# Chunk inverses on diagonal blocks of 64, one piece of expert weights split ahead, last residual by an accumulating DMA

## The chip, the core and the metric

The kernel runs on one core of a Trainium2 chip. The metric is the device time of one execution in microseconds. Before the change it is 3314.12 us, the median of 3 runs (3313.49 to 3316.09). The core has TensorE (PE; its weight loads are listed apart as PEld), VectorE (DVE), ScalarE (ACT), GpSimd (POOL) and SyncE (SP, which issues most transfers).

## The reference, cut to what matters

Two blocks run one after the other on 512 tokens of width 1024: the first has two layers (mixers, cross-attention, a gated feed-forward), the second a mixer and a layer of 32 experts. The change touches the RWKV mixer of the first block, and the start and the end of the expert layer.

```python
def rwkv7_chunked(r, log_w, k, v, a_vec, b_vec):
    ...
    A_ab = pair(a_dec, b_inv, strict)      # strictly lower triangle, inside one chunk
    A_ak = pair(a_dec, k_inv, strict)
    A_rb = pair(r_dec, b_inv, incl)
    A_rk = pair(r_dec, k_inv, incl)
    rhs = jnp.concatenate([a_dec, jnp.einsum('bhnls,bhnsv->bhnlv', A_ak, v)], axis=-1)
    sol = lax.linalg.triangular_solve(jnp.eye(L, dtype=F32) - A_ab, rhs, ...)
    ...
    def step(S, inp):                      # over the chunks, state S
        ...

def moe_ffn(h, w_router, b_router, w1, b1, w2, b2):
    logits = (xt @ w_router + b_router).astype(jnp.float32)
    top_v, top_i = lax.top_k(logits, TOP_K)
    gate = jax.nn.softmax(top_v, axis=-1)
    ...
    def expert_block(args):
        xb, e = args
        hid = xb @ w1[e] + b1[e]
        return swiglu_clamped(hid) @ w2[e] + b2[e]
    ...
# in second_block
        x = x + gate2 * moe_ffn(h2, w_router[l], b_router[l], w1[l], b1[l], w2[l], b2[l])
    return rms_norm_2(x, normf_w)
```

## The kernel before, in words

Everything is emitted by one program whose order on each engine is fixed when it is built: `merge` (L276) draws from generators in proportion to the weights that stand beside them, and the framework then places the instructions on the engines. On each engine they run in that order, and each waits for what it needs.

**The RWKV mixer.** Its 8 heads are handled in 4 pairs, p = 0 to 3. `rwkv_front(p)` makes the decayed operands `adec`, `binv`, `kinv`, `rdec` (128 partitions, 64 for each head of the pair, 512 tokens wide) from three dense products with streamed weights (`acc<-x,whi` and `acc<-x,wlo`). `rwkv_back(p)` (L773) turns them into the output. While the back of pair p runs, the front of pair p+1 is merged into it; the back of pair 3 is merged with the keys and values of the cross-attention (`mem_kv`; its products are `acc<-mp,...` and `pv<-...,mp`).

The kernel works on chunks of 64 tokens. A tile of 128 tokens holds two chunks, so a 128x128 matrix of products between the tokens of a tile has two wanted 64x64 blocks on its diagonal; the rest is removed by masks. The triangular solve is done by an inverse of (I - A) built up by doubling, for each of the two heads e of the pair apart:

- `pair` (L788): four products of 64 partitions, 128x128 each, give A (`Am`) and its transpose; both are copied by a mask into X and P, which start as identities.
- Five levels l: `prod` (L799) is four products of 128x128. Q = (Am P) masked on DVE (L846), P += X Q (L852), and, but for the last level, X += Q X (L854). So a level has two chains, one for each head, that run in turn on PE and DVE.
- `rest` (L825) is other work of the back that `next(rest, None)` hands out between the levels: `pA<-adec,kinv`, `pv`, `pA<-rdec,...`.
- Then pz = P R for each head (`pp<-R,XP`), ACT copies it out, and seven state steps (`pS`), `pw`, `py` and a norm follow.

**The expert layer.** Weights come as pieces of 128x2048 (1 MB). A piece is split into `whi` (a cast on ACT) and `wlo` (a subtraction on DVE), by `halves` (L2012); `prepare(n)` (L2024) splits until n pieces stand ready. `early` (L1938) calls `prepare(2)` after the routing and before the first tokens have been gathered and turned into `xh` and `xl`. PE multiplies a piece in 12 matmuls (`hid<-whi,xh`, `hid<-whi,xl`, `hid<-wlo,xh`, four of each kind; the down products `y` likewise). `run` (L2129) chains the instructions of PE, DVE and ACT in the order in which they are written.

**The end.** The results of experts 0 to 29 have been added to `zD` in DRAM by scatters on POOL; the results of 30 and 31 are spread to the tokens by selection matrices S. `residual` (L2214) loads the residual `xrD` and `zD` for four tiles of 128 tokens. `sums` (L2228) multiplies `zD` by the gate `g2B` on DVE. `begin` (L2274) starts a PSUM tile: residual times identity, output biases by the gates, expert 30. `gather_late` (L2290) adds expert 31 and then adds the PSUM tile to the multiplied `zD` on DVE (L2296). `norm` (L2325) squares, takes the root, scales and stores. `begin` runs for tiles 0 to 2 before the result of expert 31 is there, and for tile 3 after the first `gather_late`.

Of the kernel before, what the change touches and what calls it, by code (L numbers as in the profile page):

```python
# [182 lines left out]
def constants():  # L183
# [14 lines left out]
    for l in range(6):  # L198
# [3 lines left out]
        lev.append(off.astype(np.float32))  # L202
    A["cm"] = np.ascontiguousarray(np.concatenate(
        [ident, bones, bsw, m_incl, m_incl_sw, m_strict_sw, lev[0]] + [x.T for x in lev], axis=1))
    seg = np.ones((128, 512), np.float32)
    seg[:, ::64] = 0.0
    A["seg64"] = seg
# [74 lines left out]
class Net:  # L282
# [363 lines left out]
    def rwkv_lora(self):  # L646

        nc, A = self.nc, self.A
        self.vz = []
        for j in range(2):  # L650
            t = self.per.tile([128, 4, 192], F32, name=f"vz{j}")
            nc.gpsimd.memset(t[:, :, 64:128], 0.0)
            self.vz.append(t)
        self.wa2, self.wg2, self.lr, self.sgl = self.four("lora")
        self.yb = self.four("y")
        nc.sync.dma_start(self.wa2, A["rw_wa2"])
        nc.sync.dma_start(self.wg2, A["rw_g2"])
        lr = self.shift(self.dense(A["w_ab"], 8, 8, self.x), self.v("mu_lr1"), "lr", self.lr)
        nc.scalar.activation(lr[:64], lr[:64], AF.Tanh)
        yield 5  # L660
        sgl = self.shift(self.dense(A["w_ab"], 9, 8, self.x), self.v("mu_lr2"), "sgl", self.sgl)
        nc.scalar.activation(sgl, sgl, AF.Sigmoid)
        yield 5
# [109 lines left out]
    def rwkv_back(self, p, d, y):  # L773
# [9 lines left out]
        idb = b4(self.ident)  # L783
        rr = [slice(64 * e, 64 * e + 64) for e in range(2)]
        hc = [slice(64 - 64 * e, 128 - 64 * e) for e in range(2)]
        tiles = [slice(i * 128, i * 128 + 128) for i in range(4)]
# [9 lines left out]
            TT(t4(t), t4(ps), b4(self.c(mask)), op=OP.mult)  # L796
            return t

        def prod(x, z):  # L799
            ps = self.px("pp")  # L800
            for s in tiles:
                self.mm(ps[:, s], x[:, s], z[:, s])
            return ps


        Am, X, P = [], [], []
        inv = self.four("XP")
        pairs = self.four("Arb")
        for e in range(2):
            x, pt_ = inv[2 * e:2 * e + 2]  # L810
            nc.scalar.copy(t4(x), idb)
            nc.scalar.copy(t4(pt_), idb)
            ps = pair(e, adec, binv)
            am = self.f("Am")
            nc.scalar.copy(am, ps)
            nc.vector.copy_predicated(t4(x), b4(self.c("lev0").bitcast(I32)), t4(ps))
            ps = pair(e, binv, adec)
            nc.vector.copy_predicated(t4(pt_), b4(self.c("levt").bitcast(I32)), t4(ps))
            Am.append(am)
            X.append(x)  # L820
            P.append(pt_)
            yield 1.7
        Arb, Ark = [None, None], [None, None]

        def rest():  # L825
# [13 lines left out]

        rest = rest()  # L840
        for l in range(1, 6):
            Q = [None, None]
            for e in range(2):
                pq = prod(Am[e], P[e])
                Q[e] = self.f("Q")
                TT(t4(Q[e]), t4(pq), b4(self.c("levt", l)), op=OP.mult)  # L846
                yield 0.9
            for e in range(2):
                pp = prod(X[e], Q[e])
                if l < 5:  # L850
                    px = prod(Q[e], X[e])
                TT(P[e], pp, P[e], op=OP.add)  # L852
                if l < 5:
                    TT(X[e], px, X[e], op=OP.add)  # L854
                yield 1.7
                next(rest, None)
        for _ in rest:
            yield 0.9
        Z = []
        ZS = self.f("ZS")  # L860
        for e in range(2):
            pz = prod(P[e], R[e])
            z = self.f("Z")
            nc.scalar.copy(t4(ZS)[:, :, rr[e]], t4(pz)[:, :, rr[e]])
            nc.scalar.copy(z, pz)
            for c in range(2):
                nc.scalar.copy(ZV[rr[c], :, c, hc[e]], t4(pz)[rr[c], :, hc[e]])
            Z.append(z)
            yield 0.9
# [1049 lines left out]
class Moe:  # L1919
# [18 lines left out]
    def early(self):  # L1938

        self.wctx = ExitStack()  # L1940
        self.ctx.push(self.wctx)
        self.w = [self.wctx.enter_context(self.tc.tile_pool(name=f"mw{j}", bufs=1, side="right")) for j in range(2)]
        self.pieces = 0
        self.ready = []
        self.prepare(2)

    def open(self):
        nc, A = self.nc, self.A
# [196 lines left out]
    def experts(self):  # L2145
# [46 lines left out]
        acc, z = self.residual()  # L2192
        first = self.spread(ys[30][1], where[0])
        add = [[lambda i=i: self.sums(z[i])] for i in range(4)]
# [5 lines left out]
        p = [self.begin(i, acc[i], gT[0], first) for i in range(3)]  # L2200
        last = self.spread(self.scaled(31, sl[31], y)[1], where[1])
        norm = None
        for i in range(4):
            if i == 1:
                p.append(self.begin(3, acc[3], gT[0], first))
# [8 lines left out]
    def residual(self):  # L2214

        nc = self.nc
        t = [self.big("xr") for _ in range(5)]
        acc = [t[i // 2][:, i % 2 * 1024:i % 2 * 1024 + 1024] for i in range(4)]
        z = [t[3 + i // 2][:, i % 2 * 1024:i % 2 * 1024 + 1024] for i in range(4)]
        self.nf = t[2][:, :1024]  # L2220
        for i in range(4):
            nc.sync.dma_start(acc[i], self.n.xrD[i * 128:i * 128 + 128])
# [3 lines left out]
        return acc, z  # L2226

    def sums(self, z):  # L2228
        self.nc.vector.tensor_tensor(z, z, self.g2, op=OP.mult)

    def results(self, zD, i, big):
        z = [t for _ in range(2) for b in (big("z"),) for t in (b[:, :1024], b[:, 1024:])]
# [38 lines left out]
            self.split(hi[:, s], lo[:, s], ys[:, s])  # L2271
        return S, hi, lo

    def begin(self, i, xr, gT, late):  # L2274

        if i in (1, 2):
            pool, tag = ((self.py, "y"), (self.pt, "pt"))[i - 1]
            p = [pool.tile([128, 512], F32, tag=tag, name="pz") for _ in range(2)]
        else:
            p = self.ph.tile([128, 1024], F32, tag="hid", name="pz")  # L2280
            p = [p[:, :512], p[:, 512:]]
        S, hi, lo = late
        for o, s in zip(p, (slice(0, 512), slice(512, 1024))):
            self.mm(o, self.ident, xr[:, s], True, False)
            self.mm(o, gT[:96, i * 128:i * 128 + 128], self.b[1][:96, s], False, False)
            self.mm(o, S[:, i, :], hi[:, s], False, False)
            self.mm(o, S[:, i, :], lo[:, s], False, False)
        return p
# [51 lines left out]
def emit(ctx, tc, A, upto="all", dbg=None):  # L2340
# [26 lines left out]
    N.early()  # L2367
    N.clear(N.zD, N.big("zero"))
    for p in range(4):
        back = (N.rwkv_back(p, d[p], y), 45)  # L2370
        if p < 3:
            merge(back, (N.rwkv_front(p + 1, d[p + 1]), 27))
        else:
# [62 lines left out]
```

## Time and profile before

| | |
|---|---|
| median of 3 runs | 3314.12 us |
| the profiled execution: its own time | 3308.96 us |
| its span | 3307.1 us |
| PE busy | 3216.8 us (97%) |
| DVE busy | 2347.8 us (71%) |
| ACT busy | 1832.9 us (55%) |
| RWKV backs of the four pairs, from their first product to the end of the last inverse | about 160 to 460 us of the span |
| expert layer | about 2098 to 3274 us of the span |

The span is the time from the first to the last instruction; the 1.9 us beside it lie around it. Busy time of matmuls is modelled at their ends, so the distance between the starts of one block and the next is a better price than the length of a row. fp32 matmuls leave two records each: 160 products `pp<-Q,XP` of 128x128 stand as x320. Rows name tiles by their output and inputs and carry the line of the helper that recorded them (L348 is `mm` of the first block, L1981 that of the expert layer).

### The profile page before, as it was taken

Reading aid. Unit: us, or ns where it says so; the run is one execution under the profiler, and the core shown is the slowest. Engines: PE = TensorE matmul, PEld = TensorE weight load, DVE = VectorE, ACT = ScalarE, POOL = GpSimd, SP = SyncE. Lnnn points to the kernel's source line nnn. Section 1 sums busy time; section 2 is a strip of 40 time slices with the busy share of each in tenths; the row PEclk is TensorE's granted clock in tenths of the full one; section 3 lists DMA queues with packets and bytes.
Section 4 is the critical chain, followed back from the end, with each engine's and each line's share of the span. In section 5 each row is a group of like instructions: output and inputs, shape, how many; then the busy total and the mean of one; then the engine's idle time right before and its main releaser. Section 6 shows DMA issues by size and latency. Waiting matters only on the chain. (4 is left out here: it accounts for less than half of the span.)

```text
span 3307.1 us, 40569 instructions
## 1 busy us (share of the span) xinstructions
PE 3216.8 (97%) x15334; PEld 2564.3 (78%) x15335; DVE 2347.8 (71%) x3023; ACT 1832.9 (55%) x2356; POOL 205.4 (6%) x139
## 2 busy tenths in 40 slices
PE   8999999999999999999999998899999999999997
PEld 6688887777876787777877765688888888788885
DVE  5677765577634665577634354799999999999997
ACT  6643334443425864443434355577777777777774
POOL 1000001100000001100011000100110010111000
PEclk9999999999999999999999999899999999999999
DMA  5201123344333234345334312799999999999994
GB/s 167 79 20 29 43 89 121 122 168 169 90 125 111 75 118 126 126 147 184 90 110 135 128 50 105 275 355 360 366 366 366 353 358 367 359 358 357 369 358 161
DMA packets 152967, 649.61 MB, mean 196 GB/s; under 512 B 21335, under 2 KB 26543, under 8 KB 103228
## 3 DMA queue, kind: packets, MB, share of 16 engines
q1 hardware_dynamic: 143836, 630.86, 52.3%
q0 software_dynamic: 8928, 16.09, 1.9%
q8 instruction: 122, 2.00, 0.2%
q14 instruction: 81, 0.66, 0.1%
HBM read 626.55 MB, written 36.75 MB: 201 GB/s over the span
## 5 line engine op out<-in xcount | busy, mean ns | idle before, releaser
L1990 DVE TENSOR_TENSOR wlo<-w,whi 128x2048 fp32r<-128x2048 f32 x384 | 868.2, 2288 | 81.2 <-ACT whi L1989 76.5
L1989 ACT CAST whi<-w 128x2048 fp32r<-128x2048 f32 x384 | 729.7, 1908 | 295.9 <-PE hid L1981 178.5
L348 PE MATMUL acc<-x,whi 128*128 128x512 f32 (+1 forms) x2656 | 861.9, 404 | 7.2 <-ACT x L420 2.6
L383 ACT CAST whi<-raw 128x512 fp32r<-128x512 f32 (+1 forms) x578 | 352.8, 613 | 727.8 <-PE acc L348 600.6
L384 DVE TENSOR_TENSOR wlo<-raw,whi 128x512 fp32r<-128x512 f32 (+1 forms) x578 | 394.2, 685 | 389.8 <-ACT whi L383 373.5
L348 PEld LDWEIGHTS acc<-x,whi 128*128 128x128 f32 (+1 forms) x2656 | 496.1, 188 | 155.3 <-issue 25.4
L348 PE MATMUL acc<-x,wlo 128*128 128x512 f32 (+1 forms) x1328 | 534.0, 402 | 0.0
L1981 PE MATMUL hid<-whi,xh 128*128 128x512 f32 x1024 | 412.5, 403 | 4.5 <-DVE ln L2084 4.5
L1981 PE MATMUL hid<-whi,xl 128*128 128x512 f32 x1024 | 402.5, 393 | 2.6 <-DVE xl L1990 2.6
L348 PEld LDWEIGHTS acc<-x,wlo 128*128 128x128 f32 (+1 forms) x1328 | 250.0, 188 | 66.1 <-issue 6.3
L1981 PE MATMUL hid<-wlo,xh 128*128 128x512 f32 x1024 | 278.2, 393 | 0.0
L1981 PEld LDWEIGHTS hid<-whi,xh 128*128 128x128 f32 x1024 | 193.8, 189 | 46.2 <-issue 5.5
L1981 PEld LDWEIGHTS hid<-wlo,xh 128*128 128x128 f32 x1024 | 193.5, 189 | 42.7
L1981 PEld LDWEIGHTS hid<-whi,xl 128*128 128x128 f32 x1024 | 194.0, 189 | 41.7 <-DVE xl L1990 3.1
L1981 PE MATMUL y<-whi,ah 128*128 128x512 f32 x512 | 200.8, 392 | 0.7 <-ACT ah L1989 0.7
L1981 PE MATMUL y<-whi,al 128*128 128x512 f32 x512 | 200.3, 391 | 0.9 <-DVE al L1990 0.9
L348 PE MATMUL acc<-act,whi 128*128 128x512 f32 x512 | 162.6, 398 | 0.0
L1981 PE MATMUL y<-wlo,ah 128*128 128x512 f32 x512 | 158.8, 391 | 0.5 <-DVE wlo L1990 0.5
L455 POOL TENSOR_TENSOR sq<-sq,hs 128x512 f32<-128x512 f32 x42 | 56.2, 1339 | 1207.5 <-ACT hs L454 1207.1
L2121 POOL DMA_INDIRECT zD<-ys,sl x30 | 79.0, 2634 | 776.2 <-ACT sel L2043 466.5
L348 PEld LDWEIGHTS acc<-act,whi 128*128 128x128 f32 x512 | 95.2, 188 | 27.0 <-issue 5.1
L1981 PEld LDWEIGHTS y<-whi,ah 128*128 128x128 f32 x512 | 96.1, 188 | 22.6 <-ACT ah L1989 1.1
(651 smaller groups left out, 4653.7 us busy)
## 6 DMA issues: line engine op xcount, KB each, us to landing
w<-in_w_dram SPq DMA_DIRECT2D x384, 1024.0 KB, 8.2
raw<-in_w_up_dram SPq DMA_DIRECT2D x86, 512.0 KB, 3.5
wada<-in_w_ada_dram SPq DMA_DIRECT2D x96, 256.0 KB, 5.0
raw<-in_w_dn_dram SPq DMA_DIRECT2D x32, 512.0 KB, 3.6
h<-hD SPq DMA_DIRECT2D x48, 256.0 KB, 2.8
raw<-in_w_ab_dram SPq DMA_DIRECT2D x22, 512.0 KB, 3.6
hD<-hn SPq DMA_DIRECT2D x40, 256.0 KB, 2.0
raw<-in_w_k_dram SPq DMA_DIRECT2D x16, 512.0 KB, 3.5
```

The costliest lines, as they stand in the source:

```text
L348: self.nc.tensor.matmul(out, l, r, start=start, stop=stop)
L383: nc.scalar.copy(hi[:, :w], raw[:, c:c + w])
L384: nc.vector.tensor_tensor(lo[:, :w], raw[:, c:c + w], hi[:, :w].bitcast(F32), op=OP.subtract)
L455: nc.gpsimd.tensor_tensor(self.sq, self.sq, s, op=OP.add)
L1981: self.nc.tensor.matmul(out, l, r, start=start, stop=stop)
L1989: self.nc.scalar.copy(hi, src)
L1990: self.nc.vector.tensor_tensor(lo, src, hi.bitcast(F32), op=OP.subtract)
L2121: self.nc.gpsimd.indirect_dma_start(out=self.n.zD, out_offset=bass.IndirectOffsetOnAxis(ap=sl[:, 0:1], axis=0), in_=ys, in_offset=None, bo ...
```

## The change: what it does

Three edits.

1. The inverse keeps the 64x64 diagonal blocks alone, both heads side by side: one tile of 128 partitions (chunk c of a tile on partitions 64c to 64c+63) by 512 columns (8 blocks of 64: 4 tiles of head 0, 4 of head 1). A product is now 16 products of 64x64, whose operands and output lie on partitions 0 to 63 or 64 to 127 in turn; one chain takes the place of two. pz becomes 8 products of 64 partitions by 128 columns for each head. The masks come in a new small tile `cmc`, loaded in `rwkv_lora`. The weight of the back in the merge goes from 45 to 32.
2. `early` splits one piece of weights ahead in place of two.
3. The residual is no longer multiplied by the identity on PE; after `sums` has multiplied a tile, a DMA issued by POOL adds `xrD` to it.

```diff
+        t8 = lambda t: t.rearrange("p (i l) -> p i l", l=64)
+        cm = lambda j, n: self.cmc[:, 64 * j:64 * j + 64].unsqueeze(1).to_broadcast([128, n, 64])
+        cols = [slice(j * 64, j * 64 + 64) for j in range(8)]
+        half = [slice(256 * e, 256 * e + 256) for e in range(2)]
+        def pair_c(x, z):
+            ps = [self.px("pA") for _ in range(2)]
+            for i in range(4):
+                for c in range(2):
+                    t = slice(128 * i + 64 * c, 128 * i + 64 * c + 64)
+                    for e in range(2):
+                        self.mm(ps[e][rr[c], cols[i]], x[rr[e], t], z[rr[e], t])
+            return [t[:, :256] for t in ps]
-        def prod(x, z):
+        def prod_c(x, z):
             ps = self.px("pp")
-            for s in tiles:
-                self.mm(ps[:, s], x[:, s], z[:, s])
+            for s in cols:
+                for c in range(2):
+                    self.mm(ps[rr[c], s], x[rr[c], s], z[rr[c], s])
             return ps
...
         for l in range(1, 6):
-            Q = [None, None]
-            for e in range(2):
-                pq = prod(Am[e], P[e])
-                Q[e] = self.f("Q")
-                TT(t4(Q[e]), t4(pq), b4(self.c("levt", l)), op=OP.mult)
-                yield 0.9
-            for e in range(2):
-                pp = prod(X[e], Q[e])
-                if l < 5:
-                    px = prod(Q[e], X[e])
-                TT(P[e], pp, P[e], op=OP.add)
-                if l < 5:
-                    TT(X[e], px, X[e], op=OP.add)
-                yield 1.7
-                next(rest, None)
+            pq = prod_c(Am, P)
+            Q = self.f("Q")
+            TT(t8(Q), t8(pq), cm(2 + l, 8), op=OP.mult)
+            yield 0.9
+            next(rest, None)
+            pp = prod_c(X, Q)
+            if l < 5:
+                px = prod_c(Q, X)
+            TT(P, pp, P, op=OP.add)
+            if l < 5:
+                TT(X, px, X, op=OP.add)
+            yield 1.7
+            next(rest, None)
...
         for e in range(2):
-            pz = prod(P[e], R[e])
+            pz = self.px("pp")
+            for i, s in enumerate(tiles):
+                for c in range(2):
+                    self.mm(pz[rr[c], s], P[rr[c], cols[4 * e + i]], R[e][rr[c], s])
...
-        self.prepare(2)
+        self.prepare(1)
...
-    def sums(self, z):
+    def sums(self, z, i):
         self.nc.vector.tensor_tensor(z, z, self.g2, op=OP.mult)
+        self.nc.gpsimd.dma_start(out=z, in_=self.n.xrD[i * 128:i * 128 + 128], accum_op=OP.add)
...
-            self.mm(o, self.ident, xr[:, s], True, False)
-            self.mm(o, gT[:96, i * 128:i * 128 + 128], self.b[1][:96, s], False, False)
+            self.mm(o, gT[:96, i * 128:i * 128 + 128], self.b[1][:96, s], True, False)
...
-        back = (N.rwkv_back(p, d[p], y), 45)
+        back = (N.rwkv_back(p, d[p], y), 32)
```

How the order moves is shown at three places. In the order the sizes are those of the output, and xN counts instructions (an fp32 matmul is one here).

PE, second and third level of pair 0, before (`pp<-XP,Am` is Am P, `pp<-Q,XP` is X Q, `pp<-XP,Q` is Q X; `pn` is work of the front of pair 1, `pA` and `pv` are `rest`):

```order
L348 MATMUL pv<-vz_332,aak 128x128 x4
L348 MATMUL pp<-XP,Am 128x128 x8
L348 MATMUL pp<-Q,XP 128x128 x4
L348 MATMUL pp<-XP,Q 128x128 x4
L348 MATMUL pn<-k2s,cm 128x512
L348 MATMUL pA<-adec,kinv 128x128 x4
L348 MATMUL pp<-Q,XP 128x128 x4
L348 MATMUL pp<-XP,Q 128x128 x4
```

The same place now:

```order
L351 MATMUL pv<-vz_332,aak 128x128 x4
L351 MATMUL pp<-XP,Am 64x64 x16
L351 MATMUL pA<-adec,kinv 128x128 x4
L351 MATMUL pp<-Q,XP 64x64 x16
L351 MATMUL pp<-XP,Q 64x64 x16
L351 MATMUL pn<-k2s,cm 128x512
L351 MATMUL pv<-vz_332,aak 128x128 x4
L351 MATMUL pp<-XP,Am 64x64 x16
```

Where products of one head stood between Am P and X Q of the other, there is now a product of `rest`.

DVE at the start of the expert layer, before (`di` is the last result of the routing, `wlo` a piece of weights, `xl` the first tokens):

```order
L1888 CAST di<-ds 128x16
L1990 TENSOR_TENSOR wlo<-w,whi 128x2048 x2
L1964 MEMSET meps 128x1
L1990 TENSOR_TENSOR xl<-pt,xh 128x512 x2
L1990 TENSOR_TENSOR wlo<-w,whi 128x2048
L2303 TENSOR_REDUCE mxc<-cnt 1x1
```

The same place now:

```order
L1907 CAST di<-ds 128x16
L2009 TENSOR_TENSOR wlo<-w,whi 128x2048
L1983 MEMSET meps 128x1
L2320 TENSOR_REDUCE mxc<-cnt 1x1
L2009 TENSOR_TENSOR xl<-pt,xh 128x512 x2
L2009 TENSOR_TENSOR wlo<-w,whi 128x2048 x3
```

One piece has moved from ahead of the tokens to behind them, and a small reduction the other way.

PE at the end, one half of a `begin`, before:

```order
L1981 MATMUL pz<-xr,ident__78 128x512
L1981 MATMUL pz<-b_16468,gT 128x512
L1981 MATMUL pz<-yh,S 128x512
L1981 MATMUL pz<-yl,S 128x512
```

The same place now:

```order
L2000 MATMUL pz<-b_16866,gT 128x512
L2000 MATMUL pz<-yh,S 128x512
L2000 MATMUL pz<-yl,S 128x512
```

The identity is gone from all eight halves; the order of DVE there is the same as before.

## Rows read from the trace of the kernel before

**Rows 1.** The page, part 1: busy time of each engine.

```profile
PE 3216.8 (97%) x15334; PEld 2564.3 (78%) x15335; DVE 2347.8 (71%) x3023; ACT 1832.9 (55%) x2356; POOL 205.4 (6%) x139
```

**Rows 2.** By stretches: width, then busy us of each engine, clock, DMA.

```profile
160.00:465.00 305.00, 299.88 (x2193) 263.20 (x2192) 212.25 (x372) 114.38 (x207) 0.00 (x0) 1.00 0.13 40
2060.00:3240.00 1180.00, 1161.06 (x5356) 955.87 (x5355) 1080.40 (x853) 859.48 (x676) 120.26 (x66) 0.99 0.92 353
```

**Rows 3.** What PE waited for, 160 to 465 us: total, times, longest.

```profile
PE pp L348 <- DVE Q L846: 2.3, 1, 2.3
```

**Rows 4.** Groups on PE by shape, 160 to 465 us: busy us, mean ns.

```profile
L348 PE MATMUL pp<-Q,XP 128*128 128x128 f32 x320 | 44.8, 283 | 2.3 <-DVE Q L846 2.3
...
L348 PE MATMUL pp<-R,XP 128*128 128x128 f32 x64 | 8.3, 278 | 0.0
```

**Rows 5.** Timeline of PEld inside pair 0: start us, us, what.

```profile
186.89 1.87 PEld L348 LDWEIGHTS pp<-XP,Am 128*128 128x128 f32 x16
188.68 0.19 PEld L348 LDWEIGHTS acc<-x,wlo 128*128 128x128 f32 x1
```

**Rows 6.** Timeline of PEld at products of 64x64, three places, 88 to 229 us.

```profile
88.58 0.85 PEld L348 LDWEIGHTS pkv<-vt,ket 64*64 64x64 f32 x28 [0.37 <-ACT ket L557]
...
95.01 0.31 PEld L348 LDWEIGHTS po<-qd,S 64*64 64x64 f32 x8
...
228.10 1.06 PEld L348 LDWEIGHTS py<-reff,S 64*64 64x64 f32 x20
```

**Rows 7.** Instructions on the tile po: ns min/median/max.

```profile
L348 PEld LDWEIGHTS po<-qd,S x112: 129/133/135, 92.7 to 157.1; 64*64 64x64 f32 x112
```

**Rows 8.** Timeline of PEld at a change of shape, 173 to 175 us.

```profile
173.65 0.96 PEld L348 LDWEIGHTS pA<-adec,kinv 64*128 64x128 f32 x8
...
174.73 0.97 PEld L348 LDWEIGHTS pp<-Q,XP 128*128 128x128 f32 x8
```

**Rows 9.** Timeline from a product to the next level's, 177 to 179.5 us.

```profile
177.41 1.87 PEld L348 LDWEIGHTS pp<-XP,Am 128*128 128x128 f32 x16
...
178.61 0.69 DVE L846 TENSOR_TENSOR Q<-pp,cm 128x512 f32<-128x512 f32 x1 [1.09 <-PE pp L348]
```

**Rows 10.** Timeline at the start of the expert layer, 2096 to 2107.5 us.

```profile
2096.24 4.49 DVE L1990 TENSOR_TENSOR wlo<-w,whi 128x2048 fp32r<-128x2048 f32 x2
2097.36 1.32 ACT L1989 CAST xh<-pt 128x512 fp32r<-128x512 f32 x2 [4.81 <-PE pt L2007]
...
2101.39 0.80 PE L1981 MATMUL hid<-whi,xl 128*128 128x512 f32 x1 [2.59 <-DVE xl L1990]
...
2106.25 0.63 PE L1981 MATMUL hid<-whi,xh 128*128 128x512 f32 x1
...
2107.02 0.39 PE L1981 MATMUL hid<-whi,xh 128*128 128x512 f32 x1
```

**Rows 11.** Timeline of the end, 3272 to 3295 us.

```profile
3272.15 4.62 DVE L2229 TENSOR_TENSOR xr<-xr,g2B 128x1024 f32<-128x1024 f32 x4
...
3274.03 0.42 PEld L1981 LDWEIGHTS pz<-xr,ident__78 128*128 128x128 f32 x2
...
3274.69 0.19 PEld L1981 LDWEIGHTS pz<-b,gT 96*128 96x128 f32 x1 [0.24 <-issue]
...
3278.12 1.35 DVE L1990 TENSOR_TENSOR yl<-ys,yh 128x512 fp32r<-128x512 f32 x2
...
3283.39 0.19 PEld L1981 LDWEIGHTS pz<-yh,S 128*128 128x128 f32 x1
...
3284.27 0.69 DVE L2296 TENSOR_TENSOR xr<-xr,pz 128x512 f32<-128x512 f32 x1 [4.80 <-PE pz L1981]
...
3289.42 1.28 DVE L2296 TENSOR_TENSOR xr<-xr,pz 128x512 f32<-128x512 f32 x2 [2.89 <-PE pz L1981]
```

**Rows 12.** DMA issues: KB each, median us from issue to landing.

```profile
raw<-in_w_up_dram SPq DMA_DIRECT2D x86, 512.0 KB, 3.5
...
zD<-ys,sl POOLq DMA_INDIRECT x30, 12.2
```

More of the change, by code (lines that the diff above doesn't have):

```diff
@@ L204, in constants @@
         [ident, bones, bsw, m_incl, m_incl_sw, m_strict_sw, lev[0]] + [x.T for x in lev], axis=1))
+    A["cmc"] = np.ascontiguousarray(np.concatenate(
+        [np.concatenate([x[:64, :64], x[64:, 64:]]) for x in [ident, lev[0]] + [x.T for x in lev]], axis=1))
     seg = np.ones((128, 512), np.float32)
@@ L655, in rwkv_lora @@
         self.yb = self.four("y")
+        self.cmc = self.f("cmc")
+        nc.sync.dma_start(self.cmc, A["cmc"])
         nc.sync.dma_start(self.wa2, A["rw_wa2"])
@@ L797, in masked @@
             return t
-        def prod(x, z):
+        t8 = lambda t: t.rearrange("p (i l) -> p i l", l=64)
[11 more added lines that the diff above has]
+        def prod_c(x, z):
             ps = self.px("pp")
-            for s in tiles:
-                self.mm(ps[:, s], x[:, s], z[:, s])
+            for s in cols:
+                for c in range(2):
+                    self.mm(ps[rr[c], s], x[rr[c], s], z[rr[c], s])
             return ps
-        Am, X, P = [], [], []
         inv = self.four("XP")
+        X, P = inv[:2]
         pairs = self.four("Arb")
+        Am = self.f("Am")
+        for t in (X, P):
+            nc.scalar.copy(t8(t), cm(0, 8))
+        ps = pair_c(adec, binv)
         for e in range(2):
[L810 to L821, printed above, removed]
-            yield 1.7
+            nc.scalar.copy(Am[:, half[e]], ps[e])
+            nc.vector.copy_predicated(t8(X[:, half[e]]), cm(1, 4).bitcast(I32), t8(ps[e]))
+        yield 1.7
+        ps = pair_c(binv, adec)
+        for e in range(2):
+            nc.vector.copy_predicated(t8(P[:, half[e]]), cm(2, 4).bitcast(I32), t8(ps[e]))
+        yield 1.7
         Arb, Ark = [None, None], [None, None]
@@ L841, in rwkv_back @@
         for l in range(1, 6):
-            Q = [None, None]
-            for e in range(2):
-                pq = prod(Am[e], P[e])
-                Q[e] = self.f("Q")
-                TT(t4(Q[e]), t4(pq), b4(self.c("levt", l)), op=OP.mult)
-                yield 0.9
-            for e in range(2):
-                pp = prod(X[e], Q[e])
-                if l < 5:
-                    px = prod(Q[e], X[e])
-                TT(P[e], pp, P[e], op=OP.add)
-                if l < 5:
-                    TT(X[e], px, X[e], op=OP.add)
-                yield 1.7
-                next(rest, None)
+            pq = prod_c(Am, P)
[9 more added lines that the diff above has]
+                TT(X, px, X, op=OP.add)
+            yield 1.7
+            next(rest, None)
         for _ in rest:
@@ L2191, in experts @@
             self.fetch()
-        acc, z = self.residual()
+        z = self.residual()
         first = self.spread(ys[30][1], where[0])
-        add = [[lambda i=i: self.sums(z[i])] for i in range(4)]
+        add = [[lambda i=i: self.sums(z[i], i)] for i in range(4)]
         y = self.ph.tile([128, 1024], F32, tag="hid", name="y31")
@@ L2199, in experts @@
         self.nc.scalar.activation(t, self.g2[:, 1023:], AF.Sqrt, scale=0.0, bias=self.eps)
-        p = [self.begin(i, acc[i], gT[0], first) for i in range(3)]
+        p = [self.begin(i, gT[0], first) for i in range(3)]
         last = self.spread(self.scaled(31, sl[31], y)[1], where[1])
@@ L2204, in experts @@
             if i == 1:
-                p.append(self.begin(3, acc[3], gT[0], first))
+                p.append(self.begin(3, gT[0], first))
             self.gather_late(z[i], p[i], i, last)
@@ L2216, in residual @@
         nc = self.nc
-        t = [self.big("xr") for _ in range(5)]
-        acc = [t[i // 2][:, i % 2 * 1024:i % 2 * 1024 + 1024] for i in range(4)]
-        z = [t[3 + i // 2][:, i % 2 * 1024:i % 2 * 1024 + 1024] for i in range(4)]
+        t = [self.big("z") for _ in range(3)]
+        z = [t[i // 2][:, i % 2 * 1024:i % 2 * 1024 + 1024] for i in range(4)]
         self.nf = t[2][:, :1024]
-        for i in range(4):
-            nc.sync.dma_start(acc[i], self.n.xrD[i * 128:i * 128 + 128])
         nc.sync.dma_start(self.nf, self.A["normf"].to_broadcast([128, 1024]))
@@ L2225, in residual @@
             nc.sync.dma_start(z[i], self.n.zD[i * 128:i * 128 + 128])
-        return acc, z
-    def sums(self, z):
+        return z
+    def sums(self, z, i):
         self.nc.vector.tensor_tensor(z, z, self.g2, op=OP.mult)
+        self.nc.gpsimd.dma_start(out=z, in_=self.n.xrD[i * 128:i * 128 + 128], accum_op=OP.add)
     def results(self, zD, i, big):
@@ L2272, in spread, with begin @@
         return S, hi, lo
-    def begin(self, i, xr, gT, late):
+    def begin(self, i, gT, late):
         if i in (1, 2):
```

1 line of the change is left out of this document (removed).

## The prediction

> **What bounds the kernel now.** I read the page's busy times first: PE 97%, DVE 71%, ACT 55% [rows 1]. The average could hide stages with another limit, so the two stretches that hold the three edits come next, by windows [rows 2]. In the RWKV backs (160 to 465 us) PE is busy 299.88 of 305.00 us at clock 1.00, DVE 212. In the expert layer (2060 to 3240 us) PE is busy 1161 of 1180 us, with the DMA share at 0.92. So what comes off PE's list comes off the end, unless PE then waits. In the backs the waits of PE name one long one on the inverse, 2.3 us for a Q, once [rows 3]: two heads in turn keep it fed. Last I read the timeline of weight loads (PEld), since the distance from one block's start to the next prices a product, and the two places of edits 2 and 3.
>
> **Edit 1, what goes.** The groups by shape give each product as two records: `pp<-Q,XP` x320, pz x64 [rows 4]. By the code a pair has 112 matmuls of 128x128 in the levels (24 in four levels, 16 in the fifth), 8 for pz and 16 for A and its transpose: 136, in four pairs 544, or 1088 records. Sixteen records of Am P start at 186.89, the next block at 188.68 [rows 5]: 0.112 us each. 1088 x 0.112 = 122 us off PE.
>
> **Edit 1, what comes.** 16 matmuls of 64x64x64 for each of 14 products, and 32 for A and its transpose: 256 a pair, 1024 in all, 2048 records. pz is 64 matmuls of 64 rows by 128 columns, 128 records. A record has half the columns of the old one and there are twice as many, so this pays only if records on different parts of the array overlap. The trace has three blocks of 64x64 to price that [rows 6], the last record of each taken as 0.133 us long [rows 7]:
> - `po`, one row half and both column halves, 64 columns: (0.31 - 0.133)/7 = 25 ns a record.
> - `pkv`, all four quarters: (0.85 - 0.133)/27 = 27 ns.
> - `py`, one quarter only: (1.06 - 0.133)/19 = 49 ns.
>
> The new products alternate between two quarters, as `po` does, though on two row halves. I take 25 ns: 2048 x 25 = 51.2 us. pz, with twice the columns, at 53 ns: 6.8 us. The upper end is `py`, 49 ns.
>
> What only this change adds is PE changing between full-size and 64-row work. At such a change 8 records take 1.08 us from start to start (173.65 to 174.73 [rows 8]) where 8 x 0.112 = 0.89 is due, so 0.19 us. Along the order I count 81 changes before and 160 now: 79 x 0.19 = 15 us. Bounds: 0 (the 0.19 may be the pipeline's own) to twice that.
>
> Waits: one chain now has no other head to fill the time from Am P to X Q. From its issue end DVE still needs about 1.05 us: Am P's block of 16 records is replaced at 177.41 + 1.79, its Q of 0.69 us starts at 178.61 and, for one head, waits 1.09 us on PE [rows 9]; so the last record's drain, 0.69 of DVE and two handovers stand between the products. The new order puts `pA<-adec,kinv`, `pv` or a dense product of the front between them, most of them about 0.9 us or more, so I charge only the levels where the filler is short: 4.5 us in all. The bounds are 0 and 26 us (20 levels, each 1.05 for Q and 0.25 for P, nothing covering).
>
> DVE gets lighter: per pair 28 tensor operations of 0.69 us become 14, so it bounds nothing. ACT loses half its identity copies. The weight 32 for 45 only sets which front instructions stand between levels; it is in the counted order. The new 256 KB load of `cmc` stands on SP's queue among the first loads of weights, where SP waits for free buffers; a 512 KB load lands in 3.5 us [rows 12], so it costs 0, at most 1 us.
>
> Sum: -122 + 51.2 + 6.8 + 15 + 4.5 = **-44 us** (own bounds -56, with half the changes' price and no waits, to -33).
>
> The Trainium skill, "TensorEngine Tiling (Array Packing)", section "Restrictions and Gotchas", speaks against this: row tiles that run at one time may not share a PSUM bank. `prod_c` writes both partition halves from both row halves into one bank, while `po` uses one row half and `pkv` a bank for each, so no row here shows it. By that rule the products would run one after the other, which is the second rival. The skill's "PSUM — Partial Sum Buffer", section "PSUM bank collisions raise a hardware error", puts the collision at the same bank and the same quarter of partitions, by which the two halves are free of it.
>
> **Edit 2.** Now a second `wlo` stands on DVE ahead of `xl`: two take 4.49 us from 2096.24, and PE waits 2.59 us, until 2101.39, for `xl` [rows 10]. With one piece less, `xl` can start at 2096.24 + 2.25, or when `xh` is cast, and the first `xl` matmul at about 2099.35: 2.0 us earlier. What is late next: the second piece. ACT casts it behind `xh`, about 2098.6 to 2100.5, DVE subtracts to 2102.8, and PE has 12 matmuls of the first piece at 0.63 us before it asks, so it is covered. But PE runs at its half clock here: a matmul takes 0.63 us until 2106.25 and 0.39 from 2107.02 [rows 10]. If the clock comes back at the same moment as before, only the work done at half speed is gained, 1.0. I take **-1.5 us**, bounds 0 to -3.5.
>
> **Edit 3.** The identity takes 3274.03 to 3274.69, 0.66 us a half [rows 11]. Six halves stand before the first `gather_late`: 4.0 us. `pz<-yh` of expert 31 would start at 3283.39 - 3.96 = 3279.43; its `yl` is done at 3278.12 + 1.35 = 3279.47, so this just fits. DVE, which waited 4.80 us for PE there, starts its first addition at 3280.3 in place of 3284.27. The two halves of tile 3 give 1.3 more. The path to the end is then 5.3 us shorter, if the accumulating DMAs land in time. The four multiplications end 3273.3, 3274.5, 3275.6 and 3276.8 (4.62 us from 3272.15, in four); their tiles are needed at about 3280.3, 3284.1, 3286.7 and 3289.3: 7.0, 9.6, 11.1 and 12.5 us of room. Bounds on a landing: 3.5 us (512 KB load by SP) and 12.2 us (512 KB scatter that accumulates, by POOL, beside the weights' stream) [rows 12]. At the end the weights are through, so the value is nearer the first; at the second, tile 0 is 5.2 us late and the gain is gone. SP's four loads of `xrD` go, and nothing queues behind the four issues on POOL, which is idle. I take **-5 us**, bounds +3 (the four landing one after the other) to -5.3.
>
> The total is -44 - 1.5 - 5 = -50.5. Against the profiled execution's own 3308.96 that is 3258.5; the median of the runs shown is 3314.12, 5.2 higher, so **3264 us**.
>
> **The rivals.**
> - Chain-bound: fillers don't cover the one chain, PE waits 26 us instead of 4.5. For it: P and X must be added on DVE before the next Am P, with fewer products between. Against: DVE's share falls and the order has a filler at most places. -22.5 - 6.5 = -29: 3285 us.
> - Serial quarters, slower: two records never overlap, at `py`'s 49 ns. 99.7 + 14.3 (pz at 0.112) + 15 - 122 = +7, and the wait for Q half uncovered (20 x 1.05 / 2) +10.5: +17.5, with edits 2 and 3 +11: 3325 us. Edit 1 decides for slower from about 50 ns a record with these waits, or from about 49 ns without them plus 7 us of anything else. For it: no block in the trace alternates row halves into one tile. Against: `pkv` uses all four quarters and shows 27 ns.
> - The residual lands late: edit 3 gives 0 or costs 3, and the time is 3269 to 3272. It lies inside the range.
>
> **How the numbers follow.** Forecast 0.75 (its own range 3252 to 3280, from -56 and -33 of edit 1 with the ends of the others), chain-bound 0.10, serial 0.13 (of which slower 0.08, since the price may lie between 25 and 49 ns, and no change 0.05), anything else 0.02. A difference under 0.2%, 6.6 us, is about what a measurement can't tell from none. Faster 0.75 + 0.10 = 0.85; same 0.05 + 0.01; slower 0.08 + 0.01. The range takes in the chain-bound case and some spare below for waits and changes of shape that cost nothing: 3248 to 3292; the serial case is left out.
>
> **What would show it.** The 32 records of one `prod_c` should start 25 to 27 ns apart, so a product takes about 0.8 us; at 1.6 us the serial rival has come true. PE's waits on Q, P and X over the backs should sum to a few us; 20 or more make it chain-bound. The stretch from the first product to the last inverse, about 300 us, should be shorter by some 44. PE's wait on `xl` should fall from 2.59 to under 1 us, and the first addition at the end should wait on PE or `yl`, not on a DMA. The forecast is wrong if a product of 64x64 costs as much as one of 128x128 did, or if the backs keep their length with PE idle.

## The result and the profile after

The changed kernel takes 3255.14 us (median of 4 runs, 3252.67 to 3257.53); the kernel before takes 3313.8 beside it. The ratio is 0.9822, 95% interval 0.9805 to 0.9839. The forecast was 3264 us, within 3248 to 3292. The profiled execution of the changed kernel takes 3255.70 us, with a span of 3253.8. Beside the experiments further down the kernel before took 3312.3 to 3314.6 us, so that times set side by side from different experiments can differ by some 2 us for no reason of the kernel's.

First the page's busy times and the two windows of [rows 1, 2], of the changed kernel (width, then busy us of PE, PEld, DVE, ACT, POOL; clock, DMA share, GB/s):

```profile
PE 3166.6 (97%) x16406; PEld 2505.7 (77%) x16407; DVE 2307.8 (71%) x2967; ACT 1826.8 (56%) x2348; POOL 208.9 (6%) x143
```

```profile
160.00:465.00 305.00, 303.28 (x3532) 245.85 (x3532) 204.28 (x368) 132.73 (x240) 3.57 (x3) 1.00 0.19 60
2060.00:3240.00 1180.00, 1167.55 (x5393) 960.62 (x5391) 1098.23 (x832) 868.38 (x681) 115.64 (x64) 1.00 0.92 349
```

PE stays the bound, at 97%, and the RWKV stretch is even fuller, at 303.28 us of 305. What PE waited for there, 160 to 465 us, answers to [rows 3]:

```profile
PE pS L351 <- DVE Ts L897: 0.6, 1, 0.6
PE pp L351 <- ACT whi L386: 0.5, 1, 0.5
```

Neither names Q, P or X. The timeline of the weight loads in pair 0 answers to [rows 5, 8], with the first product of the back, a block of pz and what follows it (start us, us, what):

```profile
163.95 0.56 PEld L351 LDWEIGHTS pA<-binv,adec 64*64 64x64 f32 x32 [0.22 <-PE pr L351]
...
173.67 1.01 PEld L351 LDWEIGHTS pp<-Q,XP 64*64 64x64 f32 x32 [0.36 <-issue]
174.59 1.02 PEld L351 LDWEIGHTS pp<-XP,Q 64*64 64x64 f32 x32
175.68 0.97 PEld L351 LDWEIGHTS pv<-vz,aak 128*128 128x128 f32 x8
176.77 1.01 PEld L351 LDWEIGHTS pp<-XP,Am 64*64 64x64 f32 x32
177.84 0.96 PEld L351 LDWEIGHTS pA<-adec,kinv 64*128 64x128 f32 x8
178.93 1.01 PEld L351 LDWEIGHTS pp<-Q,XP 64*64 64x64 f32 x32
...
404.03 0.85 PEld L351 LDWEIGHTS pp<-R,XP 64*64 64x64 f32 x16 [0.36 <-issue]
405.05 0.19 PEld L351 LDWEIGHTS pv<-whi,mp 128*128 128x128 f32 x1 [0.17 <-issue]
```

A product of 32 records is followed by the next after 0.92 us (173.67 to 174.59): 29 ns a record. Where the shape changes behind it, it takes 1.07 to 1.09, and 8 records of `pA` 1.09 where 0.89 is due: 0.15 to 0.20 us for each change, as an estimate from these rows. A and its transpose, on all four quarters, take 0.56 us for 32 records, or (0.56 - 0.133)/31 = 14 ns each.

The starts of the expert layer and of the end, of the changed kernel, answer to [rows 10, 11]; they are cut from the timelines of PE, PEld and DVE:

```profile
2054.70 0.79 PE L2000 MATMUL hid<-whi,xh 128*128 128x512 f32 x1
2055.97 0.79 PE L2000 MATMUL hid<-whi,xl 128*128 128x512 f32 x1 [0.47 <-DVE xl L2009]
...
2058.69 0.63 PE L2000 MATMUL hid<-whi,xl 128*128 128x512 f32 x1
...
2060.46 0.39 PE L2000 MATMUL hid<-whi,xh 128*128 128x512 f32 x1
...
3227.57 0.19 PEld L2000 LDWEIGHTS pz<-b,gT 96*128 96x128 f32 x1
...
3228.26 0.19 PEld L2000 LDWEIGHTS pz<-b,gT 96*128 96x128 f32 x1
...
3232.41 0.19 PEld L2000 LDWEIGHTS pz<-yl,S 128*128 128x128 f32 x1 [0.45 <-DVE yl L2009]
...
3232.95 0.69 DVE L2313 TENSOR_TENSOR z<-z,pz 128x512 f32<-128x512 f32 x1
...
3243.56 0.69 DVE L2313 TENSOR_TENSOR z<-z,pz 128x512 f32<-128x512 f32 x1 [1.31 <-PE pz L2000]
```

The granted clock there, by windows of the changed kernel, rises at 2060.0 from the lower of its two levels (0.50, which is 1.2 GHz) to the higher (1.00, 2.4 GHz):

```profile
2057.70:2060.00 2.30, 2.30 (x7) 1.72 (x7) 2.30 (x2) 2.23 (x3) 0.00 (x0) 0.50 0.73 310
2060.00:2063.00 3.00, 3.00 (x15) 2.48 (x14) 3.00 (x2) 1.79 (x2) 0.00 (x0) 1.00 0.81 259
```

And the rows of the kernel before that are wanted beside them: its first product of the back, its first of the experts, the third block and the second half of its first `begin`, and its last addition. `sc<-kT,q`, the first product of the cross-attention's scores, comes behind the backs and all that is merged with them; it stands here for both kernels.

```profile
160.91 0.96 PEld L348 LDWEIGHTS pA<-binv,adec 64*128 64x128 f32 x8 [0.22 <-PE pr L348]
...
541.79 0.59 PE L348 MATMUL sc<-kT,q 128*128 128x256 f32 x2
...
2098.00 0.80 PE L1981 MATMUL hid<-whi,xh 128*128 128x512 f32 x1
...
3275.12 0.19 PEld L1981 LDWEIGHTS pz<-yh,S 128*128 128x128 f32 x1 [0.24 <-issue]
...
3275.59 0.42 PEld L1981 LDWEIGHTS pz<-xr,ident__78 128*128 128x128 f32 x2
...
3296.60 0.69 DVE L2296 TENSOR_TENSOR xr<-xr,pz 128x512 f32<-128x512 f32 x1 [1.31 <-PE pz L1981]
```

```profile
497.81 0.59 PE L351 MATMUL sc<-kT,q 128*128 128x256 f32 x2
```

These marks cut the span into parts, one for each edit:

| from, to | before | after | difference |
|---|---|---|---|
| start to first product of the back | 160.91 | 163.95 | +3.0 |
| to the first product of the scores (edit 1) | 380.9 | 333.9 | -47.0 |
| to the first product of the experts (code that no edit touches) | 1556.2 | 1556.9 | +0.7 |
| to the first product of `begin` (edit 2) | 1176.0 | 1172.9 | -3.2 |
| to the last addition (edit 3) | 22.6 | 16.0 | -6.6 |

The sum of -53.1 is what the spans show (3307.1 to 3253.8), but for 0.2 behind the last addition. The +3.0 at the start is not the change's: the granted clock between 100 and 120 us, in which both levels stand, differs from one execution to the next. The windows 100 to 120 us of the changed kernel and of the run without the residual, whose code is the same up to the end of the expert layer:

```profile
100.00:120.00 20.00, 17.10 (x82) 12.46 (x81) 12.96 (x23) 11.56 (x17) 0.00 (x0) 0.74 0.02 9
```

```profile
100.00:120.00 20.00, 17.59 (x98) 13.19 (x97) 15.38 (x30) 14.35 (x23) 0.00 (x0) 0.91 0.16 52
```

The first begins its backs at 163.95, the second at 160.85. Over the eleven traces this clock goes from 0.66 to 0.91, and the backs begin between 159.92 and 164.47, in the main the later the lower it is. The profiled execution of before had 0.91, and lies 5 us under its median (3308.96 against 3313.8); the clock of this stretch would explain some 3 of them. So the parts are compared from mark to mark. Two more traces of the same inverse take 333.8 and 333.9 us to the first product of the scores, and 1555.8 and 1556.0 from there to the experts.

### The profile page after: what moved, and what is told of

It reads as the page before. It is cut to its first block, busy times and chain, and to the rows that moved or that the text cites. A ratio compares the mean times of both kernels' runs of the same rounds, so it can differ in the third digit from the quotient of the medians.

```text
span 3253.8 us, 42647 instructions
## 1 busy us (share of the span) xinstructions
PE 3166.6 (97%) x16406; PEld 2505.7 (77%) x16407; DVE 2307.8 (71%) x2967; ACT 1826.8 (56%) x2348; POOL 208.9 (6%) x143
```

## The experiments

**Edit 1 alone** (the kernel before with the new inverse, `cmc` and the weight 32). The edit is shown against the changed kernel, cut: it takes back edits 2 and 3.

```diff
-        self.prepare(1)
+        self.prepare(2)
...
+            self.mm(o, self.ident, xr[:, s], True, False)
```

> Edit 1 alone (the diagonal inverse and the merge weight), on the kernel before. In the changed kernel the first product of the experts stands 43.3 us earlier (2098.00 to 2054.70 us), all of it ahead of edits 2 and 3. Theory (edit 1 pays for itself on PE, nothing is handed back): 43 us less than before, within 3. Rival (part of those 43 us is another execution's luck and edits 2 and 3 carry more): 35 us or less.

3264.65 us, ratio 0.9854 (0.9839 to 0.9869): 48.6 us less than before. Its marks are these (the first product of the back, of the experts, and the first with `xl`):

```profile
159.92 0.56 PEld L351 LDWEIGHTS pA<-binv,adec 64*64 64x64 f32 x32 [0.22 <-PE pr L351]
...
2049.53 0.79 PE L2000 MATMUL hid<-whi,xh 128*128 128x512 f32 x1
...
2052.91 0.79 PE L2000 MATMUL hid<-whi,xl 128*128 128x512 f32 x1 [2.59 <-DVE xl L2009]
```

From its first product to that of the experts it takes 1889.6, so 47.5 less than before, and the wait of 2.59 us for `xl` is there as in [rows 10]. Both are more than the 43 expected: that number had still held the 3.0 us by which the changed kernel's profiled execution begins later, and 0.7 lost in code that no edit touches. Nothing of edit 1 is handed back later, and the rival's 35 is out.

**Edits 2 and 3 alone** (the kernel before with one piece split ahead and the accumulating DMA). The edit is shown against the kernel before, cut.

```diff
-        self.prepare(2)
+        self.prepare(1)
...
+        self.nc.gpsimd.dma_start(out=z, in_=self.n.xrD[i * 128:i * 128 + 128], accum_op=OP.add)
```

> Edits 2 and 3 alone, with the old inverse. The prediction gave them 6.5 us. Theory from the trace of the changed kernel: the first product with xl comes 2.1 us nearer to the first with xh, and from the first product of the end to the last addition 6.6 us go: 8 to 10 us less than before. Rival (the prediction's sizes were right): 6 to 7 us less; if the accumulating DMA came late in other executions, 3 or less.

3302.69 us, ratio 0.9966 (0.9952 to 0.9979): 10.6 us less, where the marks give 9.6 (3.05 and 6.59). With edit 1's 48.6 that makes 59.2, and all three together give 58.7: the edits add up.

**The order in a product.** The theory of the forecast's price was that neighbours on different parts of the array overlap.

```diff
-            for s in cols:
-                for c in range(2):
+            for c in range(2):
+                for s in cols:
                     self.mm(ps[rr[c], s], x[rr[c], s], z[rr[c], s])
```

> The changed kernel, but prod_c issues the 8 products of one chunk first, and then the 8 of the other, so neighbours share a quarter of the array. Theory (the overlap comes from neighbours on different quarters): a product of 32 records goes from 0.92 us to about 32 x 0.049 = 1.56 us, 56 products, so 36 us slower than the changed kernel, about 3291 us. Rival (64x64 records cost 29 ns in any order): the same time as the changed kernel, 3255.

3293.85 us, ratio 0.9942 (0.9927 to 0.9958): 38.7 us slower than the changed kernel. The weight loads of Am P, of what follows it, and of X Q (its last two records come among the first of Q X):

```profile
178.55 1.76 PEld L351 LDWEIGHTS pp<-XP,Am 64*64 64x64 f32 x32
180.37 0.96 PEld L351 LDWEIGHTS pA<-adec,kinv 64*128 64x128 f32 x8
181.46 1.64 PEld L351 LDWEIGHTS pp<-Q,XP 64*64 64x64 f32 x30
```

With the last record taken off as in the prediction, Am P has (1.76 - 0.133)/31 = 52 ns a record and X Q (1.64 - 0.133)/29 = 52, where Am P of the changed kernel has (1.01 - 0.133)/31 = 28. The same matmuls in another order cost about what `py` in one quarter does, 49 [rows 6]. With this order edit 1 would be worth about 8 us.

**All four quarters.** Head 1's X and Q lie on the other half of the partitions than its P and Am, so that Am P and X Q go from each half to each.

```diff
+        def prod_4(x, z):
+            ps = [self.px("pp") for _ in range(2)]
+            for i in range(4):
+                for o in range(2):
+                    for e in range(2):
+                        self.mm(ps[e][rr[o], cols[i]], x[rr[o ^ e], cols[4 * e + i]], z[rr[o ^ e], cols[4 * e + i]])
...
-            pq = prod_c(Am, P)
+            pq = prod_4(Am, P)
...
-            pp = prod_c(X, Q)
+            pp = prod_4(X, Q)
```

> The changed kernel, but head 1's X and Q lie on the other partition half than its P and Am, each head's output in a PSUM tile of its own, so Am P and X Q use all four quarters in turn, as pair_c does (0.55 us for 32 records, 17 ns each). Q's mask and P's addition become two instructions of 256 columns. Theory (the more quarters in turn, the more overlap, and PE is the bound): 40 products x 32 x (28.75 - 17.4 ns) = 14.5 us less, 16 more records a pair cost 2: 12 us less than the changed kernel, about 3243. Rival (the chain through DVE is the bound by now, or the longer DVE part gives it back): the records get shorter and PE waits for Q and P instead; 0 to +5.

3241.78 us, ratio 0.9782 (0.9769 to 0.9795): 13.4 us less than the changed kernel, and 72 less than before. The weight loads of a level:

```profile
176.47 0.56 PEld L351 LDWEIGHTS pp<-XP,Am 64*64 64x64 f32 x32
177.09 0.96 PEld L351 LDWEIGHTS pA<-adec,kinv 64*128 64x128 f32 x8
178.18 0.56 PEld L351 LDWEIGHTS pp<-Q,XP 64*64 64x64 f32 x32
178.64 1.02 PEld L351 LDWEIGHTS pp<-XP,Q 64*64 64x64 f32 x32
```

X Q takes 0.46 us, 14 ns a record. Q X, which stays on two quarters, still takes 1.02 by its row. The added DVE instructions (Q's mask and P's sum in two halves of 256 columns) are hardly felt: PE's waits of 160 to 465 us sum to 2.0 where the changed kernel has 1.1. From the first product of the back to that of the scores it takes 319.1, so 14.8 less. One, two (both row halves) and four quarters in turn cost 52, 29 and 14 ns.

**Two PSUM tiles.** The two row halves of a product write to a tile of their own.

```diff
-            ps = self.px("pp")
+            ps = [self.px("pp") for _ in range(2)]
...
-                    self.mm(ps[rr[c], s], x[rr[c], s], z[rr[c], s])
+                    self.mm(ps[c][rr[c], s], x[rr[c], s], z[rr[c], s])
```

> The changed kernel, but the two row halves of a prod_c write into two PSUM tiles, each read by DVE instructions of 64 partitions, so twice as many. Read is the distance of the records. Theory (which quarters are used in turn sets the price, not the bank): 32 records stay at 0.92 us, 29 ns each. Rival (row halves that share a PSUM bank hold each other up): the block falls to 0.8 us or less, 25 ns or fewer. The time itself is to rise by DVE's added work if it is on the path.

The block, in the same place:

```profile
176.69 1.01 PEld L351 LDWEIGHTS pp<-XP,Am 64*64 64x64 f32 x32
177.77 0.96 PEld L351 LDWEIGHTS pA<-adec,kinv 64*128 64x128 f32 x8
```

1.08 us to the next block, as in the changed kernel (1.07), and the same holds for the other blocks of Am P that are issued whole: the shared tile costs nothing. The one time is 3279.43 us, 24 more, so the split itself is no gain. DVE is busy 213.7 us from 160 to 440 where it was 188.2. X Q is issued in pieces, as the halves of Q come, and its records stand 43 ns apart in the mean where the changed kernel has 28: some 8 to 9 us over its 20 blocks. That would be so if the records of one half run for a stretch without the other's, which no row shows. The granted clock is 0.50 from 347.9 to 354.7, which it is not at this place in the changed kernel. That this is all of the 24 us was not tried.

**No filler between Q and X Q.**

```diff
             yield 0.9
-            next(rest, None)
             pp = prod_c(X, Q)
```

> The changed kernel without the next(rest) between Q and X Q, so a product of rest stands only once a level; the rest of it comes after the levels. Theory (the merged front covers the gap as well, PE waits 1.1 us in all in the backs of the changed kernel): PE's waits on Q, P and X rise by at most 5 us, time +0 to +4. Rival (the single chain is held together by this filler alone): about 1 us of wait in each of 16 to 20 levels, +10 to +20.

3249.22 us, ratio 0.981 (0.9794 to 0.9826): 5.9 us less by the medians, and 4 by the ratios, whose intervals overlap (the changed kernel has 0.9805 to 0.9839). By the marks it is 4.6 us to the experts, and 5.1 to the first product of the scores (328.8 for 333.9), where traces of one inverse agree within 0.1. Both theories had it equal or slower. What PE waited for, 160 to 465 us:

```profile
PE pT L351 <- ACT ZS L882: 1.1, 1, 1.1
PE pA L351 <- DVE rt L645: 0.5, 1, 0.5
```

Q, P and X are not among it: the merged front covers the chain alone. I counted along the weight loads, from the first product of the back to the last `py`, how often the operand's shape changes: 172 times in the changed kernel, 145 here (84 before the change). At the 0.15 to 0.20 us of the rows 27 changes are 4.0 to 5.4 us, which would be the difference. That fits, but no run alters the changes of shape alone.

**The weight 45.**

```diff
-        back = (N.rwkv_back(p, d[p], y), 32)
+        back = (N.rwkv_back(p, d[p], y), 45)
```

> The changed kernel with the merge weight of the back left at 45, so the back is drawn at another pace against the front. Theory (PE has work of either kind at all times, the weight only sets which): within 4 us of the changed kernel, 3251 to 3259. Rival (the weight is what hides the chain, its share of edit 1 is real): 8 us or more slower.

3262.88 us, ratio 0.9844 (0.9828 to 0.9861): 7.7 us slower by the medians, 7.4 by the marks to the experts, 6.4 to the first product of the scores (340.3). The intervals of the ratios overlap, so the marks decide. That is between the two expectations, nearer to the rival's. Nine waits of PE, 160 to 465 us, take the place of two; the first four:

```profile
PE pm L351 <- ACT y L941: 1.5, 1, 1.5
PE pm L351 <- DVE yl L934: 1.4, 1, 1.4
PE pT L351 <- ACT ZS L883: 1.1, 1, 1.1
PE pt L740 <- DVE adec L722: 1.0, 1, 1.0
```

They sum to 7.9 us with the last five, against 1.1. One of 0.7 is on a tile of the inverse (`XP`), the others are on the state, the norm and the front. Behind the two longest the granted clock falls, which it does not at this place in the changed kernel:

```profile
351.20:358.00 6.80, 5.29 (x6) 1.89 (x7) 3.92 (x8) 2.94 (x7) 0.00 (x0) 0.50 0.01 2
```

PE had waited about 3 us of the 11 before (busy 7.95 from 340 to 351, at 1.00). Two records of `pm` take 2.08 us in it, and 1.12 in the changed kernel at 1.00. So 6.8 us of waits and up to 3.4 us by the clock stand against 24 changes of shape less (148 for 172; 3.6 to 4.8 us), which makes up to 5.4 to 6.6 for the 6.4 measured. So the weight's worth lies in PE's finding work at the ends of a pair.

**The residual left out** (the four accumulating DMAs are gone, so the sum lacks `xrD`).

```diff
-        self.nc.gpsimd.dma_start(out=z, in_=self.n.xrD[i * 128:i * 128 + 128], accum_op=OP.add)
```

> The changed kernel without the four accumulating DMAs: the residual is left out of the sum. Read is the distance from the first product of begin to the first and to the last addition of the end, 5.38 and 15.99 us in the changed kernel. Theory (the DMAs land in time): both stay within 0.5 us. Rival (the landing sets the first addition: 7.7 us in the median from issue, 5.2 at least, with 5.5 us of room): the first addition comes 1 us or more sooner.

First product of `begin`, first and last addition:

```profile
3223.92 0.40 PE L2000 MATMUL pz<-b,gT 96*128 96x512 f32 x1
...
3229.07 0.69 DVE L2312 TENSOR_TENSOR z<-z,pz 128x512 f32<-128x512 f32 x1
...
3239.68 0.69 DVE L2312 TENSOR_TENSOR z<-z,pz 128x512 f32<-128x512 f32 x1 [1.32 <-PE pz L2000]
```

5.15 and 15.76 us. In the changed kernel the same product is at 3227.79 on PE, so 5.16 and 15.77 (the 5.38 and 15.99 of the expectation count from its weight load). So the DMAs cost nothing in these two executions, though in the changed kernel's view of DMA issues they take longer than the 3.5 us of [rows 12]:

```profile
z<-xrD POOLq DMA_DIRECT2D x4, 512.0 KB, 7.7
```

The shortest of the four takes 5.2 us, the longest 9.8; the first is issued at 3227.47 and its tile is wanted at 3232.95, 5.5 us later. The room is small for the first tile: a landing of 6 us would be felt.

**Four quarters and no filler.**

```diff
             yield 0.9
-            next(rest, None)
             pp = prod_4(X, Q)
```

> Both improvements together: the four quarters in turn (13.4 us faster than the changed kernel) and no next(rest) between Q and X Q (5.9 us faster by the medians, 4.65 us by the stretch from the first product of the backs to the first of the experts). Theory (the filler cost changes of shape, 30 fewer of them; the two gains add up): 18 us less than the changed kernel, about 3237 us. Rival (with products of 0.46 us the front no longer covers the wait for Q, so the filler was worth its price there): 3242 or more, with PE waiting on Q.

3240.05 us, ratio 0.9775 (0.9762 to 0.9789), against 0.9782 (0.9769 to 0.9795) with the filler: no difference that can be told. The changes of shape fall from 169 to 140, but PE's waits of 160 to 465 us rise from 2.0 to 3.6, the largest of them now on the inverse:

```profile
PE pp L351 <- DVE XP L853: 1.3, 1, 1.3
...
```

From the first product of the back to that of the scores it takes 317.0 us, four quarters with the filler 319.1: 2.1 us less. To the first of the experts it is 1877.5 against 1876.1, so 3.5 us are lost between, in code that does not differ (1560.5 us against 1557.0; the other traces have 1555.8 to 1559.5). At 0.15 to 0.20 us, 29 changes should be worth 4.4 to 5.8 us, and the new waits give back 1.6; what is left over the 2.1 stays open. Either version beats both kernels.

## Why the prediction was right, and where its sizes were off

The mechanism was right: PE is the bound before and after, the 64x64 products overlap, and what comes off PE's list comes off the end. By the marks the three edits give 47.0, 3.2 and 6.6 us, together 56.8, where 50.5 stood; by the medians it is 58.7. Of the signs named, PE's waits in the backs (1.1 us) and its wait on `xl` (0.47) came as said, and no wait on a DMA is seen at the end; the records stand 29 ns apart where 25 to 27 were named. From the first product to the end of the last pz it takes 244.9 us for 298.9, so 54 less where some 44 stood; from there to the first product of the scores it takes 7 more, so that 47.0 stay. That the sum comes so near is in part luck: the records were priced 4 us too low and the waits 8 us too high, and the two errors partly cancel.

- **The price of a record.** 25 ns was taken from `po`. `prod_c` has 29, on two row halves, so its 1792 records cost 51.5 us; the 256 of A and its transpose cost at least 3.6 at 14 ns, in place of 51.2 for all. So the term was 4 us too small. That `po`, with one row half and both column halves, and `pkv` with all four at 27 ns could stand for it was near enough, but `pkv` did not show what four quarters in turn can do: its records have twice the columns.
- **The waits, and a weight priced at nothing.** I added 4.5 us for the single chain, and put the weight 32 for 45 at nothing beyond the order. The rows show 1.1 us of waits in 160 to 465 us where the kernel before had 4.9, so 8 us better than charged. With the weight left at 45 they show 7.9, which is 3.0 more than before, but only 0.7 of that names the inverse. So the single chain cost almost nothing at either weight, and the weight that was put at nothing is worth 6.4 of the 47.0 us of edit 1. The chain-bound rival is out at either weight, and the filler on which I let the cover rest was not what covered: without it there is no wait for the chain either, at records of 29 ns. At 14 ns one of 1.3 us appears.
- **The changes of shape** were not measured alone: -122 + 51.5 + 3.6 + 6.8 - 3.8 leaves about 17 us for the measured -47.0, where 15 were charged for 79 changes; the trace shows 88 more, 0.19 us each. pz was right: 16 records and the change behind them take 1.02 us.
- **The bounds.** The forecast's own range, 3252 to 3280, does not follow from the ends it names: -56, -3.5 and -5.3 give 3249, and -33, 0 and +3 give 3284. The -33 is not worked out either; twice the price of the changes and waits of 26 us would give more. The range of 3248 to 3292 held all the same.
- **The serial rival** had its price about right (52 ns measured, 49 taken) and its condition wrong: the two row halves write to one tile and overlap (29 ns against 52), and tiles of their own change nothing. The Trainium skill, "TensorEngine Tiling (Array Packing)", section "Restrictions and Gotchas", does not let different row tiles access one PSUM bank at one time. The trace does not agree: both halves write to one tile at 29 ns a record. The Trainium skill's "PSUM — Partial Sum Buffer", section "PSUM bank collisions raise a hardware error", quotes that rule too, but has two writes from different row tiles collide at the same bank and the same quadrant of partitions. The trace agrees with that: the halves write to different partitions, and no delay is seen (1.07 us a block, 1.08 with two tiles).
- **Edit 2** gave 3.2 us, in its bounds but twice the value taken. The first `xl` product comes 1.27 us after the first `xh` in place of 3.39, so 2.1 sooner where the forecast had 2.0. I had let the clock come back at its old moment, and so counted 1.0 of them; it came back earlier, 5.3 us after the first `xh` product in place of 8.9 (at 2060.0, and before at 2106.9), so that all 2.1 stayed and 0.7 came on top. In the nine traces with this edit it is 4.8 to 6.2, in the two without it 8.7 and 8.9. PE had not waited since 2055.97 when it rose, and before not since 2101.39. In the rows, the last of 0.63 shown and the first of 0.39 stand 4.0 and 5.8 us behind the first product (2054.70 to 2058.69 and 2060.46); before it was 8.3 and 9.0 (2098.00 to 2106.25 and 2107.02 [rows 10]). The last 0.3 come with a second stretch of 0.50, 3.4 us long from 2087.3 where before it was 6.8 from 2130.8.
- **Edit 3** gave 6.6 us where the forecast had at most 5.3. Half a `begin` goes from 1.56 us (3274.03 to 3275.59) to 0.69 (3227.57 to 3228.26). I had priced the identity from its start to the next block's, 0.66, which holds the gap of 0.24 behind it [rows 11]; a second gap of 0.24, one block later at 3275.12, went as well. The step "0.66 us a half" was mis-sized and is 0.87, which for eight halves is 7.0. The 0.45 us that PE now waits for `yl` is the tie that was foreseen, and leaves the 6.6. The landing was foreseen between 3.5 and 12.2 us, and is 7.7.
- **From the profiled execution to the median** 5.2 us were added, which is right for a forecast of the median. Some 3 of them are the better clock that the profiled execution of before had at 100 to 120 us. Against that execution the sum gave 3258.5, near the measured 3255.14, but that is chance: from median to median the change is 58.7 us, and the forecast was 8 short. The marks explain 56.8 of it; the other 2 lie within the spread of either kernel's times.

## What to carry to other kernels

Small matmuls pay by the order in which they are issued: here the same 64x64 products cost 52, 29 or 14 ns a record with one, two or four quarters of the array in turn, so lay the operands out so that neighbours use different quarters. Count the changes of shape as well as the products, at an estimated 0.15 to 0.20 us each here. Look for a wait on a chain before a filler is put into it: without the filler the changed kernel lost 5.1 us, and the one on four quarters 2.1 up to the scores and nothing in its whole time. Price the weights of a merge as well: one number was worth 6.4 us. An edit at one place is best read from mark to mark in the trace, since two executions of the same code began their backs 3 us apart.

## What the runs showed of the hardware

Products on the two row halves of the array that write to one PSUM tile in turn, in different partitions, are not slowed by it: 1.07 us for a block with its change of shape, 1.08 with two tiles. With four quarters in turn (the run of that name) each tile is also written from both row halves, at 14 ns a record. Two gaps of 0.24 us stood on the weight loads behind each identity, the second a whole block later, so that its removal was worth 0.87 us a half where its own block has 0.66. From 100 to 120 us the granted clock was between 0.66 and 0.91 over eleven traces, and 0.74 and 0.91 in two executions of identical code up to there; the one with the lower began the backs 3.1 us later. At the start of the expert layer the return from 0.50 to 1.00 came 4.8 to 6.2 us after the first product in the nine traces with one piece split ahead, and 8.7 and 8.9 in the two with two.
